# A planner with measured costs for issues and landings, residuals in attention's tiles, and weights cast two ahead, in a two-layer encoder trunk

## The chip, the cores and the metric

The kernel runs on one core of a Trainium2 chip. The metric is device time in microseconds of one execution, lower is better. TensorE (PE) multiplies, VectorE (DVE), ScalarE (ACT) and GpSimd (POOL) do the rest; nearly all transfers are issued by SyncE (SP) into one DMA queue, in its order.

## The reference, cut to what matters

Two sequences (2048 and 512 tokens, width 1024, float32) go through two layers with the same weights.

```python
def even_sublayer(x, w_in, ...):
    u = x @ w_in
    qa, ka, va, za, gd, qb, kb, vb, zb = jnp.split(u, _offsets(EVEN_SPLITS), axis=-1)
    ya = gla_mixer(qa, ka, va, za, gd, ...)    # gated linear attention, both directions, 4 heads of 128
    yb = swa_mixer(qb, kb, vb, zb, ...)        # |i - j| <= 128, 8 query heads, 2 key heads of 64
    return jnp.concatenate([ya, yb], axis=-1) @ w_out

def odd_sublayer(x, w_in, conv_w, w_out):
    u = x @ w_in
    bg, cg, h, z = jnp.split(u, 4, axis=-1)
    t = jnp.pad(cg * h, ((0, 0), (1, 1), (0, 0)))
    conv = conv_w[0] * t[:, :-2] + conv_w[1] * t[:, 1:-1] + conv_w[2] * t[:, 2:]
    return (jax.nn.silu(z) * bg * conv) @ w_out

# each layer
x = layer_norm(DN_ALPHA * x + sub, ln_g[l], ln_b[l])
```

## The kernel before

The 2560 tokens are five groups of 512 (group 4 is the short sequence). A product in float32 precision is made of three products of a rounded format: activations and weights are each split into a high and a low part (`xh`, `xl`; `wh`, `wl`), and xh·wh + xl·wh + xh·wl goes into one PSUM bank (`acc`).

**The dense stream** is TensorE's backbone: stages e1 (input projection of the even layer, 8 weights `w_tok` and 21 weights `w_ch`), oe (its output projection, 8 weights `w_oe`, then residual and LayerNorm to `x1_s`) and odd (32 weights `w_od`, the convolution, 8 weights `w_oo`, residual and LayerNorm to the output). Their order is e1 of groups 4, 3, 2, 1; oe 4; e1 0; odd 4; oe 0; oe 1; odd 0; oe 2; odd 1; oe 3; odd 2; odd 3. A weight tile is 128x1024 and serves 24 matmuls of 512 columns. It is loaded into `ws` (two buffers), cast to its high part `wh` by ScalarE, and the low part `wl` is subtracted by GpSimd in four pieces:

```python
    def cook(self):
        ...
            hi = self.new(self.wp, (128, 1024), F32R, "wh", 2)[:, :n]
            lo = self.new(self.wp, (128, 1024), F32R, "wl", 2)[:, :n]
            nc.scalar.copy(hi, raw)
            for o in range(0, n, n // 4):
                ...
            self.cooked.append((hi, lo))
            self.fetch()

    def weight(self):
        ...
        w = self.cooked.pop(0)
        self.cook()
        return w
```

`weight()` is called where a weight's matmuls begin, so the cast of the next one and the load (`fetch`) of a further one are written there. The load has to wait until the subtraction has read the buffer, and it waits at the head of SP's queue.

**Side streams** are generators that are stepped between groups of dense matmuls (at each `yield` of the dense code, by `Flow.pump`): `prep` and `prep_odd` load a group's activations (`pr`, two buffers), transpose them where needed and split them into `st`; `gla_stream` runs the linear attention in chunks of 128 tokens (tiles `qn`, `tA`, `KK`, `QQ`, `S`, `A`; loads from `k_s`, `q_s`, `qf_s` and so on); `swa_front` and `swa_back` run the windowed attention (`P`, `Q`, `K`, `V`, `mx`, `pth`, `ptl`); `norms` does LayerNorms. PSUM has eight banks: four `acc` for the dense stream, one `psg` for the linear attention, three `pss` for the windowed attention and the transposes.

**The order** of all instructions is fixed when the kernel is built. A small model (`Model`) keeps a clock for every engine, with a cost for each instruction and a landing time for each DMA; a stream's next step is written when the model's TensorE clock has passed the time at which its input is reckoned ready and VectorE and ScalarE are not more than some microseconds ahead. The model's numbers place instructions; on the chip semaphores decide. An instruction placed too early makes its engine wait, with all that stands behind it.

**Residuals and LayerNorm gains.** In `out_ln`, a side stream added where the projection starts waits for the previous projection's LayerNorms, loads gain and offset (`lnf`, `lnb`) and then four or five residual tiles `y` (four buffers, which the LayerNorms before it still use). VectorE adds a finished bank to the residual (`half`), which frees the bank.

Almost every instruction carries line 188, that of the helper which records it; the profile is read by tile names.

Of the kernel before, what the change touches and what calls it, by code (L numbers as in the profile page):

```python
# [96 lines left out]
class Model:  # L97


    def __init__(self):  # L100
        self.clock = dict.fromkeys(("tensor", "vector", "scalar", "gpsimd", "sync"), 0.0)
        self.bus = 0.0
        self.written, self.used, self.free, self.rings = {}, {}, {}, {}
        self.last = 0.0
        self.by, self.dram, self.held = {}, set(), set()

# [10 lines left out]

    def idle(self, name):
        return max(self.written.get(name, (0.0, ""))[0], self.used.get(name, 0.0))

    def alloc(self, tag, old, tile):
        ring = self.rings[tag]
        name = tile.tensor.name
        if old is not None:
            ring.remove(old)
            self.free[name] = self.idle(old)
        ring.append(name)

# [3 lines left out]
    def cost(self, engine, op, outs, ins):  # L132
        n = max(x.free_size() for x in outs + (ins if op != "matmul" else []))
# [6 lines left out]
        if engine == "vector":  # L140
            return n / 960 + 0.155, 0.06
        if engine == "scalar":
            return n / 1250 + 0.21, 0.06
        return n / 480 + 0.3, 0.06

    def note(self, engine, op, outs, ins):
# [21 lines left out]
        for x in outs:  # L168
            if x.tensor.name not in self.dram:
                self.written[x.tensor.name] = (end, engine)  # L170
# [38 lines left out]
class Flow:  # L209
# [5 lines left out]
    AHEAD = 5.0  # L215

    def __init__(self, model):
# [4 lines left out]
        self.late = []  # L222
# [8 lines left out]
    def add(self, gen, ready=0.0):  # L231
        self.side.append([self.t + ready, self.n, gen, None])
        self.n += 1
# [4 lines left out]

    def flush(self, everything=False, name=None):
# [3 lines left out]
        self.late = keep  # L243
# [3 lines left out]
    def drain(self):  # L247
        while self.late:
            self.flush(True)

    def step(self, s):
# [8 lines left out]
        try:  # L260
# [3 lines left out]
            return  # L264
        s[0] = max(self.t, self.model.last)
# [4 lines left out]
        elif said:  # L270
            s[0] = max(s[0], self.model.when(said))

    def room(self):
        c = self.model.clock
        return c["vector"] <= self.t + self.AHEAD and c["scalar"] <= self.t + self.AHEAD - 1.5

    def pump(self):
        self.flush()
        for s in sorted(self.side, key=lambda s: s[:2]):
            if s[0] <= self.t and self.room():  # L280
# [34 lines left out]
class Trunk:  # L315
    def __init__(self, tc, nc, I, y_out, ctx):
# [13 lines left out]
        self.psg = P("psg", 1, space=PSUM)  # L330
        self.pss = P("pss", 3, space=PSUM)
# [18 lines left out]
        self.up_made = False  # L350
# [5 lines left out]
        self.jobs, self.raws, self.cooked = [], [], []  # L356
# [16 lines left out]
    def pd(self, shape=(128, 512), dt=F32):  # L373
        return self.new(self.acc, shape, dt, "acc", 4)

    def pg(self, shape=(128, 512), dt=F32):
        return self.new(self.psg, shape, dt, "psg", 1)

    def pw(self, shape=(128, 512), dt=F32, hold=False):
        return self.new(self.pss, shape, dt, "pss", 3, hold)  # L380

    def m2(self, shape=(128, 512), dt=F32, hold=False):
        return self.new(self.md, shape, dt, "md", 4, hold)
# [6 lines left out]


    def fetch(self):

        if self.jobs:
            src, n = self.jobs.pop(0)
            raw = self.new(self.wp, (128, 1024), F32, "ws", 2)[:, :n]
            self.nc.sync.dma_start(raw, src)
            self.raws.append((raw, n))

    def cook(self):  # L400

        nc = self.nc
        if not self.raws:
            self.fetch()
        if self.raws:
            raw, n = self.raws.pop(0)
            hi = self.new(self.wp, (128, 1024), F32R, "wh", 2)[:, :n]
            lo = self.new(self.wp, (128, 1024), F32R, "wl", 2)[:, :n]
            nc.scalar.copy(hi, raw)
            for o in range(0, n, n // 4):  # L410
                c = slice(o, o + n // 4)
                nc.gpsimd.tensor_tensor(lo[:, c], raw[:, c], hi[:, c].bitcast(F32), op=ALU.subtract)
# [16 lines left out]
    def dense_ch(self, xh, xl):  # L429
# [4 lines left out]
        for k in range(8):  # L434
# [3 lines left out]
            yield  # L438
        for k in range(8):
            c = slice(k * 128, k * 128 + 128)  # L440
            nc.tensor.matmul(p[:], wl[:, c], xh(k), start=False, stop=(k == 7))
            if k % 2 and k < 7:
                yield
        return p

    def dense_tok(self, n, tiles, put):

        nc = self.nc
        out = [(self.pd() if i < 4 else self.pw())[:, :n] for i, t in enumerate(tiles)]
        for kc in range(4):  # L450
# [13 lines left out]
            for i, ((xh, xl), p) in enumerate(zip(tiles, out)):  # L464
                yield from high(xh, xl, p)
                if kc == 3:
                    low(xh, p)
                    put(i, p)
                    yield
            if kc < 3:  # L470
                for (xh, xl), p in zip(tiles, out):
                    low(xh, p)
                    yield

    def log_sig(self, z, out):
# [5 lines left out]
        nc.vector.scalar_tensor_tensor(out, z, 0.0, out, op0=ALU.min, op1=ALU.subtract)  # L481

    def silu(self, z, out, tile, g=None, then=None):

        nc = self.nc
        self.log_sig(z, out)
# [12 lines left out]
        self.flow.defer(rest, tile, z)  # L499
# [26 lines left out]
    def setup_up(self):  # L526

        nc, I = self.nc, self.I
        up = self.new(self.yp, (128, 2, 512), F32R, "y", 4)
        if self.up_made:  # L530
            nc.sync.dma_start(up[:].bitcast(F32), self.up_s)
            return up
        self.up_made = True
# [3 lines left out]
        for d, n in enumerate("bf"):  # L537
            nc.sync.dma_start(raw[:, d], I["up_" + n])
        for d in range(2):
            lo = low[:, d]  # L540
            nc.scalar.copy(hi[:, d], raw[:, d])
# [4 lines left out]
        nc.sync.dma_start(self.up_s, up[:].bitcast(F32))  # L546
        return up

    def setup_late(self):
        nc, c = self.nc, self.const  # L550
# [3 lines left out]
        self.sink = load("sink", (128, 8))  # L554
        self.nsink = c.tile([128, 8], F32, name="nsink")
        nc.vector.tensor_scalar(self.nsink[:], self.sink[:], -1.0, None, op0=ALU.mult)
        self.lmask16 = load("m16", (128, 32), I32)

    def setup_bias(self):
        nc, I, c = self.nc, self.I, self.const  # L560
        self.setup_late()
# [20 lines left out]
        self.bias = c.tile([128, 8, 384], F32, name="bias")  # L582
        b = self.bias_s
        yield 6.0
        nc.sync.dma_start(self.bias[:], bass.AP(b.tensor, b.offset + 127, [[511, 128], [65536, 8], [1, 384]]))
# [6 lines left out]
    def prep(self, key, src, gates):  # L592
# [8 lines left out]
        def get(k):  # L601
            r = self.new(self.md, (128, 512), F32, "pr", 2, True)
            nc.sync.dma_start(r[:], src(k))
            raws.append(r)

        get(0)
        get(1)
        for k in range(8):
            yield raws[:1]
# [9 lines left out]
            if k < 6:  # L619
                get(k + 2)  # L620
        self.flow.mark(key)

    def prep_odd(self, g, gates):
# [10 lines left out]
        def get(hf, t):  # L634
            r = (4 * g + t) * 128
            y = self.new(self.md, (128, 512), F32, "pr", 2, True)
            nc.sync.dma_start(y[:], self.x1_s[r:r + 128, hf * 512:hf * 512 + 512])
            raws.append(y)

        get(*jobs[0])  # L640
        get(*jobs[1])
        for i, (hf, t) in enumerate(jobs):
# [5 lines left out]
            while not self.model.spare("pss", 3):  # L648
                yield 0.5
# [6 lines left out]
            if i < 6:  # L656
                get(*jobs[i + 2])
# [18 lines left out]
    def e1(self, g):  # L676
# [8 lines left out]
        gd = self.sm((128, 4, 32), "gd")  # L685

        def put_v(t, p):
            v = self.m2()
            nc.scalar.copy(v[:, :336], p)
            flow.defer(lambda: nc.sync.dma_start(self.v_s[4 * g + t, :, :336], v[:, :336]), v)  # L690

        def put_r(t, p):
# [6 lines left out]
            nc.vector.tensor_tensor(mk(r, 320, [[64, 2], [1, 64]]), pv, hi, op=ALU.subtract)  # L699
# [4 lines left out]
            flow.defer(store, r)  # L704
# [724 lines left out]
```

## Time and profile before

| | |
|---|---|
| time, median of 3 runs | 2770.91 us (2761.58 to 2774.79) |
| profiled execution | 2769.01 us, span 2767.2 us |
| granted TensorE clock, mean | 0.957 |
| PE busy | 2525.8 us (91%) |
| DVE, ACT, POOL busy | 1429.2, 1208.9, 1236.3 us |
| DMA | 460.42 MB, mean 166 GB/s |

A row of waits "PE acc <- ACT wh" says that TensorE, writing `acc`, stood idle until ScalarE had written `wh`; SPq is SP's queue of DMA issues. A timeline row gives start, duration, engine, operation, tiles out<-in and count, and in brackets the idle time before it with what ended it. Names have their buffer numbers left out.

### The profile page before, as it was taken

Reading aid. Unit: us, or ns where it says so; the run is one execution under the profiler, and the core shown is the slowest. Engines: PE = TensorE matmul, PEld = TensorE weight load, DVE = VectorE, ACT = ScalarE, POOL = GpSimd, SP = SyncE. Lnnn points to the kernel's source line nnn. Section 1 sums busy time; section 2 is a strip of 40 time slices with the busy share of each in tenths; the row PEclk is TensorE's granted clock in tenths of the full one; section 3 lists DMA queues with packets and bytes.
Section 4 is the critical chain, followed back from the end, with each engine's and each line's share of the span. In section 5 each row is a group of like instructions: output and inputs, shape, how many; then the busy total and the mean of one; then the engine's idle time right before and its main releaser. Section 6 shows DMA issues by size and latency. Waiting matters only on the chain. (4 is left out here: it accounts for less than half of the span.)

```text
span 2767.2 us, 43278 instructions
## 1 busy us (share of the span) xinstructions
PE 2525.8 (91%) x16214; PEld 2077.3 (75%) x16214; DVE 1429.2 (52%) x2704; ACT 1208.9 (44%) x2276; POOL 1236.3 (45%) x1552
## 2 busy tenths in 40 slices
PE   6988999898999888999999878997899979989998
PEld 5767778677878677777777667885788758868886
DVE  1246656577777686677866544222433245324324
ACT  2544665555556345564565423332233223333331
POOL 2444434344444343444434544554455435545553
PEclk8999999999999999999999989997999989999999
DMA  4766666474665655655466753334432443234333
GB/s 148 224 204 190 204 220 208 151 232 153 208 204 178 216 178 179 197 164 174 142 219 196 264 200 123 98 98 150 164 122 99 160 167 122 93 111 145 117 99 137
DMA packets 268721, 460.42 MB, mean 166 GB/s; under 512 B 21680, under 2 KB 150448, under 8 KB 268512
## 3 DMA queue, kind: packets, MB, share of 16 engines
q1 hardware_dynamic: 268512, 457.66, 51.2%
q8 instruction: 128, 2.10, 0.3%
q14 instruction: 81, 0.66, 0.1%
HBM read 353.23 MB, written 104.35 MB: 165 GB/s over the span
## 5 line engine op out<-in xcount | busy, mean ns | idle before, releaser
L188 POOL TENSOR_TENSOR wl<-ws,wh 128x256 fp32r<-128x256 f32 (+1 forms) x1524 | 1199.9, 818 | 1476.7 <-ACT wh L188 1320.8
L188 PE MATMUL acc<-st,wh 128*128 128x512 f32 x4240 | 1059.9, 397 | 23.1 <-ACT wh L188 16.4
L188 PEld LDWEIGHTS acc<-st,wh 128*128 128x128 f32 x4240 | 793.3, 190 | 189.3 <-ACT wh L188 19.8
L188 PE MATMUL acc<-st,wl 128*128 128x512 f32 x2120 | 554.9, 396 | 0.0
L188 PE MATMUL acc<-wh,st 128*128 128x512 f32 (+1 forms) x1760 | 441.8, 391 | 71.0 <-DVE y L188 39.4
L188 ACT CAST wh<-ws 128x1024 fp32r<-128x1024 f32 (+1 forms) x381 | 385.5, 1012 | 206.5 <-PE acc L188 146.9
L188 PEld LDWEIGHTS acc<-st,wl 128*128 128x128 f32 x2120 | 395.7, 190 | 78.9
L188 PEld LDWEIGHTS acc<-wh,st 128*128 128x128 f32 x1760 | 335.1, 204 | 125.0 <-issue 37.7
L188 DVE SCALAR_TENSOR_TENSOR md<-acc,md 128x512 f32<-128x512 f32 (+1 forms) x145 | 100.0, 691 | 375.2 <-ACT md L188 354.0
L188 PE MATMUL acc<-wl,st 128*128 128x512 f32 (+1 forms) x880 | 232.0, 385 | 5.6 <-POOL wl L188 5.6
L188 ACT ACTIVATE md<-md 128x512 f32<-128x512 f32 x360 | 226.8, 630 | 11.4 <-DVE md L188 3.6
L188 PEld LDWEIGHTS acc<-wl,st 128*128 128x128 f32 x880 | 164.3, 199 | 33.9 <-POOL wl L188 8.5
L188 ACT ACTIVATE md<-acc 128x512 f32<-128x512 f32 (+1 forms) x165 | 96.8, 596 | 188.0 <-PE acc L188 135.2
L188 DVE SCALAR_TENSOR_TENSOR y<-y,acc 128x512 f32<-128x512 f32 x78 | 53.6, 687 | 168.7 <-PE acc L188 100.5
L188 DVE TENSOR_TENSOR md<-md,acc 128x512 f32<-128x512 f32 x40 | 27.4, 686 | 196.6 <-PE acc L188 196.6
L188 DVE TENSOR_TENSOR md<-acc,md 128x512 f32<-128x512 f32 (+1 forms) x120 | 74.5, 621 | 92.6 <-PE acc L188 58.8
L188 DVE CUSTOM_DVE_ANT_0 P<-pss,bias 128x384 f32<-128x384 f32 (+1 forms) x160 | 83.7, 524 | 58.7 <-PE pss L188 58.0
L188 ACT COPY km<-KK 128x512 f32<-128x512 f32 x80 | 51.1, 639 | 140.1 <-DVE KK L188 140.0
L188 ACT CAST pth<-pss 128x512 fp32r<-128x512 f32 x112 | 65.4, 584 | 105.1 <-PE pss L188 104.9
L188 DVE TENSOR_TENSOR st<-pr,st 128x512 fp32r<-128x512 f32 x80 | 60.1, 758 | 86.4 <-ACT st L188 86.3
L188 ACT ACTIVATE P<-P,nm 128x384 f32<-128x384 f32 (+1 forms) x160 | 93.6, 588 | 10.1 <-DVE nm L188 10.0
L188 ACT CAST st<-md 128x512 fp32r<-128x512 f32 x40 | 24.8, 621 | 165.3 <-DVE md L188 165.3
(151 smaller groups left out, 2595.4 us busy)
## 6 DMA issues: line engine op xcount, KB each, us to landing
ws<-in_w_od SPq DMA_DIRECT2D x160, 512.0 KB, 3.5
ws<-in_w_ch SPq DMA_DIRECT2D x105, 512.0 KB, 3.9
ws<-in_w_oe SPq DMA_DIRECT2D x40, 512.0 KB, 4.3
ws<-in_w_oo SPq DMA_DIRECT2D x40, 512.0 KB, 3.8
ws<-in_w_tok SPq DMA_DIRECT2D x40, 336.0 KB, 3.3
K<-kb_s SPq DMA_DIRECT2D x32, 384.0 KB, 6.5
pr<-in_xT SPq DMA_DIRECT2D x40, 256.0 KB, 4.7
d_s<-md SPq DMA_DIRECT2D x40, 256.0 KB, 4.6
```

What stands on the lines that cost most here:

```text
L188: r = f(*a, **k)
```

## The change

The instructions that compute stay the same; their order, their buffers and the times at which loads are issued change.

- **Estimates** (`Model`). A DMA issue costs SP 0.45 us in place of 0.06, and its data are reckoned to land 3.6 us or more after it in place of 2.2. An operation of VectorE that reads two SBUF tiles is put behind the GpSimd operation that runs at that time (`behind`). A buffer not yet written counts as busy. Some costs differ.
- **Steps.** A stream names the tiles that its next step needs (`yield [Q]`), and is written when those are ready; before, the last operation of the step before counted. `prep`, residuals and LayerNorms go ahead of attention (`rank`), and a stream may take several steps at one point. Operations of the dense code that need another engine's result first (`taps`, `split`, stores) are deferred until it is reckoned done.
- **Weights.** `wh` has three buffers. The high part of a weight is cast two weights ahead, in the middle of a weight's matmuls, the low part at the start of the next weight; the load for a free `ws` buffer is written when the model reckons it free (`fetch_soon`).
- **Residuals.** One stream (`residuals`) loads them stages ahead into any free tile of `y` and, once attention is done with them, `P`, `Q`, `tA`, `QQ`, `KK`. Gain and offset stay in `ln_g`, `ln_b`, and once attention is done in `P` and `Q` too. `pr` has three buffers, and `gb`, `pth`, `ptl` are used for the same purpose at the end of attention; `md` has eight in place of four.
- **PSUM.** `psg` and `pss` become one pool `ps` of four banks; a step waits in the plan until one is reckoned free (`bank`). The dense stream takes a bank of it when its own four are busy.
- The scratch for DMA descriptors is set to 2048 bytes (`dynamic_dma_scratch_size`).

```diff
         if engine == "sync":
-            c[engine] = at + 0.06
+            c[engine] = at + 0.45
             size = max(x.partition_size() * x.free_size() for x in outs) * 4
-            self.bus = max(self.bus, at) + size / 280e3
-            end = max(at + 2.2, self.bus + 1.6)
+            self.bus = max(self.bus, at + 0.45) + size / 280e3
+            end = max(at + 3.6, self.bus + 1.8)
         else:
             cost, more = self.cost(engine, op, outs, ins)
+            if engine == "vector":
+                at = self.behind(at, op, outs, ins)
+            elif engine == "gpsimd":
+                self.pool = self.pool[-12:] + [(at, at + cost)]
...
-    AHEAD = 5.0
+    AHEAD = ((5.0, 5.0), (4.0, 4.0), (4.0, 4.0))
...
-        self.psg = P("psg", 1, space=PSUM)
-        self.pss = P("pss", 3, space=PSUM)
+        self.pside = P("pside", 4, space=PSUM)
...
+    def fetch_soon(self):
+        ...
+        old = self.model.next_free("ws", 2)
+        self.flow.at(self.model.idle(old), go)
+
     def cook(self):
         if not self.raws:
-            self.fetch()
+            if self.coming:
+                self.coming[0]()
+            else:
+                self.fetch()
         if self.raws:
             raw, n = self.raws.pop(0)
-            hi = self.new(self.wp, (128, 1024), F32R, "wh", 2)[:, :n]
-            lo = self.new(self.wp, (128, 1024), F32R, "wl", 2)[:, :n]
-            nc.scalar.copy(hi, raw)
+            hi = self.new(self.wp, (128, 1024), F32R, "wh", 3, True)[:, :n]
+            self.nc.scalar.copy(hi, raw)
+            self.cooking.append((raw, hi, n))
+
+    def cook_low(self):
+        while self.cooking:
+            raw, hi, n = self.cooking.pop(0)
+            lo = self.new(self.wp, (128, 1024), F32R, "wl", 2, True)[:, :n]
             for o in range(0, n, n // 4):
...
             self.cooked.append((hi, lo))
-            self.fetch()
+            self.drop(raw)
+            self.fetch_soon()
 
     def weight(self):
-        if not self.cooked:
-            self.cook()
-        w = self.cooked.pop(0)
-        self.cook()
-        return w
+        self.cook_low()
+        return self.cooked.pop(0)
...
+    def residuals(self, plan):
+        for key, gates, rows, src in plan:
+            for gate in gates:
+                yield gate
+            for i, r in enumerate(rows):
+                while self.free_at(self.large) > self.flow.t or self.model.bus > self.flow.t + 1.0:
+                    yield 0.4
+                y = self.take(self.large, (128, D))
+                self.nc.sync.dma_start(y[:], src[r * 128:r * 128 + 128])
```

What the order becomes, at three places on which the prediction rests. First the start of the program. On SP (loads of the first weights and of x) there stood:

```order
L188 DMA ws<-in_w_tok 128x672
L188 DMA pr<-in_xT 128x512 x2
L188 DMA ws<-in_w_tok 128x672
L188 DMA ident<-in_ident 128x128
L188 DMA hl<-in_hl 128x2
L188 DMA norm_g<-in_norm_g 128x1
L188 DMA ws<-in_w_tok 128x672
L188 DMA pr<-in_xT 128x512 x6
L188 DMA ws<-in_w_tok 128x672 x2
```

and now:

```order
L225 DMA ws<-in_w_tok 128x672
L225 DMA pr<-in_xT 128x512 x2
L225 DMA ws<-in_w_tok 128x672
L225 DMA pr<-in_xT 128x512
L225 DMA md<-in_xT 128x512 x5
L225 DMA ident<-in_ident 128x128
L225 DMA hl<-in_hl 128x2
L225 DMA norm_g<-in_norm_g 128x1
L225 DMA ws<-in_w_tok 128x672 x2
```

The last five loads of x go into `md` tiles, ahead of the constants and of the third weight. On ACT at the same place (casts of weights and of x, before and now):

```order
L188 CAST st<-pr 128x512
L188 CAST wh<-ws 128x672
L188 CAST st<-pr 128x512 x7
L188 CAST wh<-ws 128x672 x4
L188 COPY md<-acc 128x336 x4
```

```order
L225 CAST wh<-ws 128x672
L225 CAST st<-pr 128x512 x3
L225 CAST wh<-ws 128x672
L225 CAST st<-md 128x512 x5
L225 CAST wh<-ws 128x672 x2
```

The second weight's cast moves from behind eight casts of x to behind three; the first stands ahead of all.

Second, SP around the end of odd 4 and the projection oe 0 (`in_x` is the residual of the even layer, `mix_s` the output of attention). Before, the residuals stand inside oe 0, behind the stores of odd 4's LayerNorms:

```order
L188 DMA ws<-in_w_oe 128x1024
L188 DMA out_y<-y 128x1024
L188 DMA pr<-mix_s 128x512
L188 DMA mix_s<-KK 512x1x128
L188 DMA pr<-mix_s 128x512
L188 DMA ws<-in_w_oe 128x1024
L188 DMA out_y<-y 128x1024 x2
L188 DMA lnf<-in_ln_g 128x1024
L188 DMA lnb<-in_ln_b 128x1024
L188 DMA y<-in_x 128x1024 x4
L188 DMA ws<-in_w_oe 128x1024
```

Now residuals go out from the end of odd 4 on, into `P` and `tA`, between the weights:

```order
L225 DMA QQ<-qf_s 128x512
L225 DMA qn<-ga_s 128x512
L225 DMA P<-in_x 128x1024 x2
L225 DMA ws<-in_w_oe 128x1024
L225 DMA ptl<-mix_s 128x512
L225 DMA mix_s<-KK 512x1x128
L225 DMA P<-in_x 128x1024
L225 DMA ws<-in_w_oe 128x1024
L225 DMA mix_s<-qn 512x1x128
L225 DMA pr<-mix_s 128x512
L225 DMA tA<-in_x 128x1024
L225 DMA ws<-in_w_oe 128x1024 x2
```

The residual loads moved ahead of the stores `out_y`, and the loads of gain and offset are gone from this place.

Third, SP at odd 2's output projection (`x_s` is `x1_s`: halves of a group for the next odd layer in `pr`, residuals in `y`). Before:

```order
L188 DMA ws<-in_w_oo 128x1024 x4
L188 DMA pr<-x_s 128x512 x4
L188 DMA ws<-in_w_oo 128x1024
L188 DMA pr<-x_s 128x512 x2
L188 DMA lnf<-in_ln_g 128x1024
L188 DMA lnb<-in_ln_b 128x1024
L188 DMA y<-x_s 128x1024 x4
L188 DMA pr<-x_s 128x512
L188 DMA ws<-in_w_oo 128x1024
L188 DMA pr<-x_s 128x512
L188 DMA ws<-in_w_oo 128x1024 x2
```

Now:

```order
L225 DMA ws<-in_w_oo 128x1024 x3
L225 DMA pr<-x_s 128x512
L225 DMA gb<-x_s 128x512
L225 DMA ws<-in_w_oo 128x1024
L225 DMA gb<-x_s 128x512
L225 DMA pth<-x_s 128x512
L225 DMA ptl<-x_s 128x512
L225 DMA pr<-x_s 128x512
L225 DMA pth<-x_s 128x512
L225 DMA ptl<-x_s 128x512
L225 DMA ws<-in_w_oo 128x1024 x4
```

The loads of x1 go into four kinds of tiles, the residuals are no longer here (they stand ahead of `in_w_oo`, in the last weights of `in_w_od`).

More of the change, by code (lines that the diff above doesn't have):

```diff
@@ L647, in prep_odd @@
             y = raws.pop(0)
-            while not self.model.spare("pss", 3):
-                yield 0.5
+            yield from self.bank()
             pt = self.pw((128, 4, 128), hold=True)
@@ L1146, in swa_back @@
             yield [V, Pt]
-            while self.model.spare("pss", 3) < 2:
-                yield 0.5
+            while self.model.spare("ps", 4) < 2:
+                yield 0.3
+            yield from self.bank()
             po = self.pw(hold=True)
@@ L1156, in swa_back @@
             for kb in range(nk):
-                while not self.model.spare("pss", 3):
-                    yield 0.5
+                yield from self.bank()
                 pt = self.pw((128, 4, 128), hold=True)
```

598 lines of the change are left out of this document (385 added, 213 removed).

## The prediction

> **What bounds the kernel now.** I read the page first, then the stages, the list of waits of TensorE, that of the DMA queue, and last the clock.
>
> ```profile
> span 2767.2 us, 43278 instructions
> PE 2525.8 (91%) x16214; PEld 2077.3 (75%) x16214; DVE 1429.2 (52%) x2704; ACT 1208.9 (44%) x2276; POOL 1236.3 (45%) x1552
> ```
>
> TensorE is busy 91%; no other engine passes 52%. The order of the changed program holds the same 13,447 matmuls, so only two things can move the span: the 2767.2 − 2525.8 = 241.4 us in which TensorE is idle, and the speed at which it runs while busy. The idle time by stage (the columns are the stretch, its length, then the busy time of PE, PEld, DVE, ACT, POOL, the granted clock, DMA share and GB/s):
>
> ```profile
> 0.00:160.00 160.00, 124.08 (x597) 103.48 (x598) 31.51 (x56) 62.30 (x98) 63.18 (x96) 0.88 0.64 201
> 160.00:1030.00 870.00, 801.25 (x7163) 666.66 (x7162) 583.16 (x1200) 471.82 (x933) 361.04 (x444) 0.96 0.62 193
> 1030.00:1560.00 530.00, 501.79 (x3720) 409.91 (x3719) 364.09 (x743) 298.00 (x678) 220.12 (x265) 0.98 0.58 189
> 1560.00:2490.00 930.00, 832.08 (x3572) 678.51 (x3571) 344.63 (x551) 292.01 (x446) 457.08 (x580) 0.94 0.41 135
> 2490.00:2767.20 277.20, 266.62 (x1170) 218.78 (x1168) 105.76 (x156) 84.78 (x123) 134.91 (x168) 0.99 0.37 125
> ```
>
> Length less PE busy gives 35.9 us idle in the first group, 68.8 and 28.2 while attention runs beside the projections, 97.9 in the stretch where only projections and LayerNorms are left, 10.6 at the end. The worst stretch is the one with the least work beside TensorE: it waits for data that is issued late, not for a full engine. What ended the idle time:
>
> ```profile
> PE acc L188 <- ACT wh L188: 43.0, 12, 11.7
> PE acc L188 <- DVE y L188: 39.4, 5, 13.6
> PE pss L188 <- DMA pr<-x_s: 38.6, 9, 8.9
> PE psg L188 <- DMA KK<-k_s: 21.7, 6, 8.3
> PE psg L188 <- DVE QQ L188: 19.1, 7, 5.0
> PE pss L188 <- DVE mx L188: 7.3, 4, 4.4
> PE psg L188 <- DMA QQ<-qf_s: 6.2, 2, 3.8
> PE acc L188 <- POOL wl L188: 5.6, 7, 1.3
> PE acc L188 <- DVE Q L188: 2.1, 1, 2.1
> SPq L188 <- POOL wl L188: 1121.3, 367, 6.1
> SPq L188 <- ACT wh L188: 683.1, 292, 10.5
> ```
>
> Each row names the engine and the tile it writes, what it waited for, the total in us, how often and the longest. The last two rows are the DMA queue's own. It stands still for 1121.3 + 683.1 = 1804 us, 65% of the span, behind a weight load whose buffer GpSimd or ScalarE still reads; what is queued behind that load (a residual, a chunk of attention) is late by as much.
>
> Clock is lost as well. This is the sum over the 37 stretches in which the granted clock stood at one half (length, then busy times):
>
> ```profile
> sum 236.58, PE 162.36 PEld 132.01 DVE 86.65 ACT 52.13 POOL 73.87; mean PE 4.39 PEld 3.57 DVE 2.34 ACT 1.41 POOL 2.00
> ```
>
> PE was busy 162.36 us there and did half as much as at full speed: 81 us lost. Idle and clock together hold 241 + 81 = 322 us, and with everything gone the span would be 2445 us.
>
> **The change, part by part.** The sum goes against the profiled execution, 2769.0 us (span 2767.2 and 1.8 around it); the median of the runs, 2770.9, lies 1.9 above it.
>
> (a) Weights, 43.0 + 5.6 = 48.6 us. Before, the cast of a weight's high part goes out when the weight before it starts; now it goes out two thirds through the weight ahead of that, into a third buffer. A weight is 24 matmuls, and undisturbed they take 192.03 / 846 = 0.227 us each, 5.4 us; the cast takes 1.0 us and the four subtractions behind it 4 × 0.82 = 3.3 us.
>
> ```profile
> 2509.05 192.03 PE acc L188 x846
> L188 POOL TENSOR_TENSOR wl<-ws,wh 128x256 fp32r<-128x256 f32 (+1 forms) x1524 | 1199.9, 818 | 1476.7 <-ACT wh L188 1320.8
> L188 ACT CAST wh<-ws 128x1024 fp32r<-128x1024 f32 (+1 forms) x381 | 385.5, 1012 | 206.5 <-PE acc L188 146.9
> ```
>
> So what may stand ahead of a cast on ScalarE before TensorE stops grows from 5.4 − 1.0 = 4.4 us to 1.8 + 5.4 − 1.0 = 6.2 us; the subtractions keep theirs, being needed two thirds of a weight later. The largest wait of the row is at the start:
>
> ```profile
> 9.37 10.86 SPq L188 DMA_DIRECT2D pr<-in_xT  x6
> 23.80 1.40 ACT L188 CAST wh<-ws 128x672 fp32r<-128x672 f32 x2
> 24.60 4.57 PE L188 MATMUL acc<-wh,st 128*128 128x336 f32 x16 [11.72 <-ACT wh L188]
> ```
>
> The six loads of x took 10.86 us to issue, since two buffers pass them on; the cast of the second weight stood behind all eight casts of x. Now all eight loads are issued before anything waits (first place below the change), and the second weight's cast stands behind three. The first load and cast can't go (6.3 us before the first matmul), and I leave 8 us for the rest, half of it for x that lands late at the start. Remain 14 of 48.6: 34.6 saved.
>
> (b) Residuals, 39.4 us. The one of 13.65 us:
>
> ```profile
> 1581.85 0.90 SPq L188 DMA_DIRECT2D out_y<-y  x2
> ...
> 1584.95 4.92 SPq L188 DMA_DIRECT2D y<-in_x  x4
> 1594.17 0.69 DVE L188 SCALAR_TENSOR_TENSOR y<-y,acc 128x512 f32<-128x512 f32 x1 [13.34 <-DMA y<-in_x]
> 1595.01 5.22 PE L188 MATMUL acc<-wh,st 128*128 128x512 f32 x14 [13.65 <-DVE y L188]
> ```
>
> The four residuals wait for the four y tiles that the last LayerNorms still write out, then for the gains; they land 9 us after the issue, and meanwhile the sums in PSUM can't be emptied. Now they are issued one stage ahead into tiles that attention has left (second place), tens of matmuls ahead of their use, and gain and offset stay resident. That is five waits whose cause is gone; I leave 2 us: 37.4 saved. VectorE is next in line there and idle enough (344.63 of 930 us busy).
>
> (c) Loads behind a standing queue: 38.6 (x1 for the odd layers), 21.7 (k) and 6.2 (q), 66.5 us. Typical:
>
> ```profile
> 2456.70 12.83 SPq L188 DMA_DIRECT2D ws<-in_w_oo  x3
> 2469.58 10.57 SPq L188 DMA_DIRECT2D pr<-x_s  x4
> 2473.78 1.09 PE L188 MATMUL pss<-ident,pr 128*128 128x128 f32 x4 [8.88 <-DMA pr<-x_s]
> pr<-x_s SPq DMA_DIRECT2D x40, 256.0 KB, 4.2
> ```
>
> Three weight loads hold the queue for 12.83 us, the transposes stand in TensorE's order as if x1 were there. The change queues a weight load only when its buffer is reckoned free, reckons 0.45 us for an issue and at least 3.6 us for a landing where it had 0.06 and 2.2, and spreads x1 over nine buffers in place of two (third place). Against the median landing of 4.2 us the new reckoning is nearly right; loads that take longer will still be awaited for 1 to 2 us. I keep a fifth, 13 us: 53.5 saved. What is moved in the queue is moved past the stores too (v, vb, out_y), and those are read a stage later.
>
> (d) The rest of the waits is 241.4 − 48.6 − 39.4 − 66.5 − 8.5 = 78.4 us; 8.5 us is the tail after the last matmul, which the change leaves alone:
>
> ```profile
> 2735.53 23.21 PE acc L188 x101
> ```
>
> This last run of matmuls ends at 2735.53 + 23.21 = 2758.7 of 2767.2. The 78.4 us are steps of attention placed before their input is there (19.1 and 7.3 above, the others under 6 each) and such things as the end of an odd stage, where the carried columns must be made first (the row of 2.1). In the new order a step is placed when its named input is reckoned done, no longer when the last operation of its stream is, and VectorE is reckoned later where GpSimd is at work. Unknown is how good that is: nothing back if the new estimates are as wrong as the old, all back at best. I take a half, 39 us: each step is covered by dense matmuls in the meantime, but the end of an odd stage has no such cover and stays. New mistakes of the order I put at 10 us, between 0 and as much as (d) held.
>
> (e) The clock. Half-clock stretches come with waits:
>
> ```profile
> 196.00:206.00 10.00, 7.70 (x94) 5.85 (x93) 3.12 (x5) 3.91 (x6) 3.52 (x4) 1.00 0.56 178
> 498.32 0.50 PE L188 MATMUL acc<-y 128*128 128x512 f32 x1 [1.51 <-ACT y L188]
> 499.75:503.16 3.41, 3.41 (x10) 2.65 (x9) 0.17 (x1) 3.35 (x10) 2.63 (x4) 0.50 0.00 0
> 1585.18:1598.84 13.66, 3.83 (x9) 3.09 (x10) 2.75 (x4) 0.00 (x0) 2.27 (x4) 0.50 0.91 367
> ```
>
> The first stretch holds 2.3 us of idle time and kept the full clock. The matmul in the second row came after 1.51 us of waiting, and the 3.41 us behind it ran at half speed. The last is the wait under (b). Waits fall from 233 (241.4 less the tail) to 14 + 2 + 13 + 39 + 10 = 78 us, to a third; as short ones remain and some of them cost clock, I keep 40% of 81 us: 48 saved; the ends are 0 and 81. The Trainium skill ("TensorE: Matmul & The Clock Gate", section "HAM oscillation — how this bites in real kernels") gives as the abstract rule "no PE-idle gaps >~3.4µs". By that rule the short waits that remain would cost no clock, and I estimate that some 20 us more would come back, still inside my forecast. The trace agrees only in part: ahead of the stretch at 499.75 stood no such gap.
>
> (f) What I cost at nothing. The side streams' four PSUM banks were one for the linear attention and three for the windowed; as one pool they let either stream run when the other has no need, and a step waits for a bank in the plan, under dense matmuls. The descriptor scratch made smaller only frees SBUF: the transfers go through the hardware queue.
>
> ```profile
> q1 hardware_dynamic: 268512, 457.66, 51.2%
> ```
>
> Sum: 34.6 + 37.4 + 53.5 + 39 − 10 + 48 = 202.5. Time 2769.0 − 202.5 = 2566; the median of the runs would put it 2 us higher, which I don't resolve.
>
> **Rivals.**
> 1. *Half of it.* The large waits go, but each is followed by a smaller one of the same stage, since TensorE comes sooner and loads then collide; (a) to (c) give half (63), (d) nothing, and the clock a quarter (20): 2769 − 83 = 2686. For it: DMA already takes 0.62 of its engines in the second stretch. Against: residuals move by a whole stage, which no estimate can spoil.
> 2. *Nearly all of it.* Only the start, the tail and three ends of odd stages (2.1 us each) remain idle, clock lost 10: 2445 + 6.3 + 8.5 + 6.3 + 10 + 1.8 = 2478. For it: no other engine is above 70% in any stretch.
> 3. *Slower: the weight buffers turn too slowly.* A raw buffer is loaded (3.5 us), cast (1.0) and subtracted (3.3), with the issue 0.4: 8.2 us, and two buffers must give a weight each 5.4 us, so 10.9 us per turn. Before, the next load stood in the queue and left the moment the buffer was free; now it leaves when the plan thinks so. If that is later by d, TensorE waits (d − 2.7) / 2 for each of the 381 weights. It has eaten the 202 us at d = 3.8 us and ends slower beyond that; d = 5 costs 438 us and gives 3004 us. Against it: a weight that is needed and not loaded is issued at once, and the plan's costs are near the rows.
>
> ```profile
> ws<-in_w_od SPq DMA_DIRECT2D x160, 512.0 KB, 3.5
> ```
>
> 4. *No change.* The order differs, the waits only move: within 0.5% (14 us, about what a measurement of this kernel can tell).
>
> **Numbers.** The forecast, 2500 to 2625, has 0.57; half of it (2625 to 2755) 0.21; nearly all (below 2500) 0.10; no change 0.04; slower 0.08. Faster is then 0.88. The range 2475 to 2690 leaves out the slower case, no change and the worst part of rival 1.
>
> **What would show it.** (a) PE <- ACT wh below 12 us; (b) the row PE <- DVE y gone; (c) PE waits on DMA below 20 us together, and the queue's waits for POOL wl far under 1121; (d) idle time of the second and third stretch halved; (e) a granted clock of 0.97 or more in the stretch that now has 0.94. I am wrong if weight loads are awaited in every stage, if the queue still stands, or if idle time moves to attention's PSUM banks, which are now one pool of four.

## The result and the profile after

The changed kernel takes 2506.15 us (median of 4 runs, 2504.23 to 2507.69) against 2770.88 us in the runs beside it (2761.58 to 2774.79): a ratio of 0.9049, interval 0.9025 to 0.9073. The profiled execution took 2504.69 us, with a mean granted clock of 0.994. First the span and the busy times, from the head of the page:

```profile
span 2502.9 us, 43603 instructions
PE 2445.0 (98%) x16214; PEld 2028.8 (81%) x16214; DVE 1456.4 (58%) x2710; ACT 1210.8 (48%) x2276; POOL 1248.2 (50%) x1552
```

TensorE is idle for 2502.9 − 2445.0 = 57.9 us in place of 241.4, so 183.5 us came back from waits. Its busy time fell by 2525.8 − 2445.0 = 80.8 us with the same number of instructions. The same stretches as before (length, then the busy times of PE, PEld, DVE, ACT, POOL, granted clock, DMA share, GB/s; the work in them is not quite the same, as everything comes earlier now):

```profile
0.00:160.00 160.00, 150.72 (x917) 126.24 (x918) 55.92 (x89) 86.85 (x136) 88.49 (x122) 1.00 0.78 243
160.00:1030.00 870.00, 842.58 (x7721) 704.41 (x7720) 618.53 (x1319) 509.69 (x1019) 381.50 (x471) 0.99 0.66 209
1030.00:1560.00 530.00, 523.14 (x3452) 431.33 (x3452) 374.26 (x701) 282.76 (x657) 261.46 (x304) 1.00 0.62 205
1560.00:2490.00 930.00, 924.17 (x4111) 763.50 (x4110) 399.40 (x591) 330.49 (x461) 516.72 (x656) 1.00 0.39 131
2490.00:2502.90 12.90, 4.37 (x20) 3.29 (x18) 8.29 (x11) 1.00 (x4) 0.00 (x0) 0.85 0.24 97
```

Idle are 9.3, 27.4, 6.9 and 5.8 us, and 8.5 at the end; before it was 35.9, 68.8, 28.2, 97.9 and 10.6. What TensorE waited for, and below it the DMA queue (total, times, longest):

```profile
PE acc L225 <- ACT st L225: 6.3, 1, 6.3
PE ps L225 <- DVE QQ L225: 6.1, 7, 3.0
PE acc L225 <- ACT wh L225: 5.0, 3, 2.4
PE ps L225 <- ACT A L225: 4.3, 1, 4.3
PE acc L225 <- DMA gb_s<-md: 4.2, 1, 4.2
PE acc L225 <- DVE K L225: 4.1, 2, 2.1
PE acc L225 <- POOL wl L225: 3.8, 5, 1.1
SPq L225 <- POOL wl L225: 1196.6, 325, 8.7
SPq L225 <- ACT wh L225: 77.3, 73, 3.6
```

The first row is the lead before the first matmul, 6.3 us as before the change. The waits for loads (x1, k, q) and for residuals are gone, from these rows and from those below them; the one DMA row is for a store (`gb_s<-md`) that is read back. The queue still stands for 1196.6 + 77.3 = 1274 us behind weight loads, 51% of the span (before 1804 us, 65%).

The clock: the sum over the seven stretches at half clock, the last of which is the tail (length, busy times):

```profile
sum 29.83, PE 20.63 PEld 17.41 DVE 14.25 ACT 11.81 POOL 13.61; mean PE 2.95 PEld 2.49 DVE 2.04 ACT 1.69 POOL 1.94
```

TensorE was busy 20.63 us there: 10 us lost in place of 81. So the 264.3 us between the spans are 183.5 of idle time, 71 of clock, and 10 that I can't assign.

### The profile page after: what moved, and what is told of

The parts are those of the page before. It is cut to its first block, busy times and chain, and to the rows that moved or that the text cites. A ratio compares the mean times of both kernels' runs of the same rounds, so it can differ in the third digit from the quotient of the medians.

```text
span 2502.9 us, 43603 instructions
## 1 busy us (share of the span) xinstructions
PE 2445.0 (98%) x16214; PEld 2028.8 (81%) x16214; DVE 1456.4 (58%) x2710; ACT 1210.8 (48%) x2276; POOL 1248.2 (50%) x1552
## 4 chain that ended last, share of the span: by engine, by line
PE 85%; DVE 6%; DMA 4%; ACT 2%; POOL 1%; issue 1%; SPq 1%; DVEq 0%; ACTq 0%; POOLq 0%
PE acc L225 71%; PE ps L225 14%; DVE KK L225 1%; DVE QQ L225 1%; POOL wl L225 1%; DVE P L225 1%; DMA ws<-in_w_ch 1%; DMA ws<-in_w_tok 1%; SPq L225 1%; ACT wh L225 1%; DVE st L225 1%; DMA qb_s<-md 0%; DVE md L225 0%; DVE y L225 0%; ACT P L225 0%
## 5 line engine op out<-in xcount | busy, mean ns | idle before, releaser
L225 PEld LDWEIGHTS acc<-st,wh 128*128 128x128 f32 x4160 | 768.3, 188 | 156.1 <-ACT wh L225 3.4
L225 PE MATMUL acc<-wh,st 128*128 128x512 f32 (+1 forms) x1648 | 387.1, 372 | 14.4 <-ACT st L225 6.3
L225 PEld LDWEIGHTS acc<-wh,st 128*128 128x128 f32 x1648 | 293.0, 190 | 59.3 <-ACT wh L225 7.2
L225 ACT ACTIVATE md<-md 128x512 f32<-128x512 f32 x315 | 197.6, 631 | 33.0 <-DVE md L225 26.3
L225 PE MATMUL acc<-wl,st 128*128 128x512 f32 (+1 forms) x824 | 207.7, 370 | 3.9 <-POOL wl L225 3.8
L225 ACT CAST pth<-ps 128x512 fp32r<-128x512 f32 x112 | 65.1, 581 | 71.1 <-PE ps L225 66.3
L225 DVE CUSTOM_DVE_ANT_0 P<-ps,P 128x384 f32<-128x384 f32 (+1 forms) x160 | 79.4, 525 | 29.9 <-PE ps L225 28.9
L225 DVE TENSOR_TENSOR ptl<-ps,pth 128x512 fp32r<-128x512 f32 x112 | 76.2, 681 | 6.3 <-ACT pth L225 6.0
L225 PE MATMUL ps<-K,Q 128*128 128x384 f32 (+1 forms) x320 | 74.1, 339 | 3.6 <-DVE mx L225 2.7
L225 DVE TENSOR_SCALAR P<-P,den 128x384 f32<-128x384 f32 (+1 forms) x160 | 73.7, 519 | 1.4
```

What stands on the lines that cost most here:

```text
L225: r = f(*a, **k)
```

## The experiments

Two theories. **A:** the lead over the loads comes from the estimates of the title (a DMA issue of 0.45 us, a landing of 3.6). **B:** it comes from where the weight loads stand in SP's queue: written when the plan reckons their buffer free (`fetch_soon`), no longer right behind the subtraction, so that other loads go ahead of them. Further theories take one part each: the residual's tiles, the casts two ahead, the PSUM pool, the rules of the plan. Each kernel ran in 3 rounds beside the kernel before. Since those runs were in four groups, on three chips, kernels are compared by their ratios; 0.0010 is 2.8 us. Kernels whose plans differ little came out at 0.8918 to 0.9054 (e7, e11, e1, e10), so a difference of some 20 us between two plans is not by itself the worth of one part.

| kernel | us | ratio | interval |
|---|---|---|---|
| after | 2506.2 | 0.9049 | 0.9025 to 0.9073 |
| e1 after, old DMA estimates | 2500.7 | 0.9022 | 0.9008 to 0.9035 |
| e10 after, all estimates old | 2507.8 | 0.9054 | 0.9032 to 0.9075 |
| e2 before, new DMA estimates | 2749.9 | 0.9916 | 0.9893 to 0.9940 |
| e3 after, weight loads written at once | 2564.0 | 0.9253 | 0.9237 to 0.9269 |
| e5 before, weight loads written later | 2655.9 | 0.9575 | 0.9545 to 0.9605 |
| e9 before, whole weight part | 2702.8 | 0.9761 | 0.9733 to 0.9788 |
| e6 after, cast one ahead | 2526.4 | 0.9104 | 0.9077 to 0.9132 |
| e4 after, few residual tiles | 2520.4 | 0.9092 | 0.9078 to 0.9106 |
| e12 after, PSUM banks split | 2529.2 | 0.9130 | 0.9115 to 0.9145 |
| e8 after, old rules of the plan | 2512.8 | 0.9053 | 0.9026 to 0.9080 |
| e7 after, steps wait for the last operation | 2475.0 | 0.8918 | 0.8887 to 0.8949 |
| e11 as e7, old DMA estimates | 2497.6 | 0.9016 | 0.8994 to 0.9038 |

### The estimates: e1, e2, e10

e1 puts the old numbers for a DMA into the changed kernel:

```diff
-            c[engine] = at + 0.45
+            c[engine] = at + 0.06
...
-            self.bus = max(self.bus, at + 0.45) + size / 280e3
-            end = max(at + 3.6, self.bus + 1.8)
+            self.bus = max(self.bus, at) + size / 280e3
+            end = max(at + 2.2, self.bus + 1.6)
```

> The changed kernel with the old estimates of a DMA alone (issue 0.06 us, landing 2.2 us and 1.6 after the bus), all else as changed. Theory A (lead): loads come in time because they are reckoned to land later, so that they are written further ahead of their use; then TensorE's waits on DMA come back, 30 to 60 us of them, with clock, and the time is 2560 to 2620 us. Theory B (queue): they come in time because weight loads no longer hold the head of the queue; then the time stays below 2525 us.

Not slower: 0.9022. One load of x1 is late by 8.0 us where none was (the waits of TensorE, largest row), and the rest makes up for it. Theory A falls for the changed kernel.

```profile
PE ps L225 <- DMA ptl<-x_s: 8.0, 1, 8.0
```

e2 does the reverse, the new numbers in the kernel before:

```diff
-            c[engine] = at + 0.06
+            c[engine] = at + 0.45
...
-            self.bus = max(self.bus, at) + size / 280e3
-            end = max(at + 2.2, self.bus + 1.6)
+            self.bus = max(self.bus, at + 0.45) + size / 280e3
+            end = max(at + 3.6, self.bus + 1.8)
```

> The kernel before with the new estimates of a DMA alone (0.45, 3.6, 1.8). Theory A: the rows of TensorE's waits on pr, KK and QQ fall from 66.5 us to below 25, the clock gains, and the time is 2670 to 2720 us. Theory B: the queue stands as before, the waits stay above 50 us and the time within 20 us of 2771.

It gains 0.8%, some 23 us, which is neither theory's figure: less than A's 50 us, and just more than B's 20. The wait for x1 stays and that for k falls from 21.7 to 3.5 us (last row), but waits for VectorE and ScalarE in attention rise. The queue's wait for `wh` is 679.0 us (before 683.1):

```profile
PE acc L188 <- ACT wh L188: 40.4, 14, 11.2
PE pss L188 <- DMA pr<-x_s: 39.6, 8, 8.7
PE acc L188 <- DVE y L188: 31.5, 6, 11.7
PE psg L188 <- DVE acmp L188: 29.2, 20, 4.8
PE psg L188 <- DMA KK<-k_s: 3.5, 3, 2.4
```

e10 sets back all estimates: e1's edit, the old costs of VectorE and ScalarE, and no delay behind GpSimd.

```diff
-            return n / 960 + (0.155 if len(outs) < 2 else 0.23), 0.06
+            return n / 960 + 0.155, 0.06
...
-                at = self.behind(at, op, outs, ins)
+                pass
```

> The changed kernel with all old numbers in the model: DMA, engine costs, and no waiting of VectorE behind GpSimd. Theory E (the measured numbers carry a part, as the change is named after them): steps are placed too early again, DVE and ACT waits of attention return, 2540 us or more. Rival S (structure does it, not numbers; the old DMA numbers alone cost nothing): 2490 to 2520 us.

0.9054, no difference from the changed kernel. With the rest of the change in place, the measured numbers bring nothing that can be seen.

### Where the weight loads stand: e3, e5, e9

e3 writes the load at once, in `cook_low`, and leaves all else:

```diff
-            self.fetch_soon()
+            self.fetch()
```

> The changed kernel, but a weight load is written at once when the last subtraction from its buffer is written, as before the change, so that it stands at the head of the queue. Theory A: loads have lead enough, time within 15 us of 2506. Theory B: the queue stands 600 us longer, waits on DMA of 30 us and more return, 2560 us or more.

0.9253, some 57 us above the changed kernel with the intervals far apart: the largest loss of any part undone. The waits of TensorE and of the queue:

```profile
PE ps L225 <- DMA pth<-x_s: 21.3, 3, 18.6
PE ps L225 <- ACT km L225: 20.9, 4, 9.3
SPq L225 <- POOL wl L225: 1453.9, 354, 8.8
SPq L225 <- ACT wh L225: 160.1, 125, 5.9
```

The queue stands 1614 us, 63% of its span of 2567.5. That is 340 us longer than in the changed kernel, where theory B had 600. A late x1 and late steps of attention are back, and TensorE is idle for 107.3 us in place of 57.9.

e5 gives `fetch_soon` alone to the kernel before, with the raw buffer held until it is subtracted:

```diff
     def cook(self):
         if not self.raws:
-            self.fetch()
+            if self.coming:
+                self.coming[0]()
+            else:
+                self.fetch()
...
-            self.fetch()
+            self.fetch_soon()
```

> The kernel before with one part of the change alone: the load of a weight is written when its buffer is reckoned free. Theory B (the place of weight loads in the queue is the main cause): TensorE's waits on DMA fall from 66 us to below 30, with clock, and the time is 2680 to 2720 us; the queue's waits for ScalarE's cast (683 us) fall to below 200. Theory C (the parts need each other: with two weight buffers a later load only makes the cast later): no faster than 2755 us, waits on ACT wh grow.

0.9575: 4.25% or some 118 of the 264 us by one call, with the hold that it needs. It went further than both theories had it.

```profile
PE acc L188 <- ACT wh L188: 53.2, 11, 9.4
PE pss L188 <- DMA pr<-x_s: 26.7, 6, 14.9
PE acc L188 <- DVE y L188: 22.2, 3, 9.8
SPq L188 <- POOL wl L188: 846.5, 309, 5.3
SPq L188 <- ACT wh L188: 486.6, 219, 13.4
```

The queue stands 1333 us, 50% of 2660.2. I expected its wait for `wh` below 200 us; it is 486.6, as the cast is still written late. The wait for k (21.7 us before) is gone, x1 and residuals have lost a third and nearly half, and the wait for `wh` itself has grown (43.0 to 53.2).

e9 adds the rest of the weight part to that: a third `wh`, the high part cast two ahead, the low part at the next weight's start, and the small descriptor scratch:

```diff
-            hi = self.new(self.wp, (128, 1024), F32R, "wh", 2)[:, :n]
+            hi = self.new(self.wp, (128, 1024), F32R, "wh", 3, True)[:, :n]
...
-        w = self.cooked.pop(0)
-        self.cook()
-        return w
+        self.cook_low()
+        return self.cooked.pop(0)
...
+                if i == 2:
+                    self.cook()
```

> The kernel before with the whole weight part of the change and nothing else: later loads, a third buffer for high parts, casts two ahead, the low part at the next weight's start. Theory Q (the queue is the main cause and the later cast adds to it): waits on ACT wh fall from 53.2 us (later loads alone) to below 25, and the time is 2600 to 2640 us. Rival (the casts matter only with the rest of the change): within 15 us of 2656, which later loads alone gave.

0.9761, some 51 us slower than e5, which neither theory had. The row that it aims at did fall, but those of attention rose:

```profile
PE psg L188 <- DVE acmp L188: 29.0, 18, 7.4
PE psg L188 <- ACT km L188: 28.8, 10, 8.7
PE acc L188 <- ACT wh L188: 20.4, 6, 6.8
1424.00:1640.00 216.00, 150.99 (x966) 117.79 (x966) 150.47 (x328) 105.71 (x343) 35.99 (x44) 0.80 0.64 209
```

The last row is a stretch as above. GpSimd, which prepares the weights, is busy for 36 of 216 us: few dense matmuls are left to place, and the last steps of attention, which oe 0 needs, run one behind the other at a granted clock of 0.80. The dense stream had come there sooner than attention. So a part that works alone can lose when another bound lies next; the queue stands only 46% here, so that share is not by itself a measure of the time.

### One part undone: e6, e4, e12

e6 has two `wh` buffers and casts a weight at the start of the one before it:

```diff
-            hi = self.new(self.wp, (128, 1024), F32R, "wh", 3, True)[:, :n]
+            hi = self.new(self.wp, (128, 1024), F32R, "wh", 2, True)[:, :n]
...
+        w = self.cooked.pop(0)
+        self.cook()
...
-                if i == 2:
-                    self.cook()
```

> The changed kernel with the cast of a weight where it was, at the start of the weight before, and two buffers for high parts. Theory W (casts two ahead carry a large part, since the later load needs the slack): waits on ACT wh and POOL wl grow from 8.8 us to 40 us or more, the clock falls, 2560 us or more. Rival, the prediction's reckoning of spare time (4.4 us against 6.2): 10 to 20 us slower, below 2530 us.

0.9104, some 15 us slower. TensorE's wait for the cast is small, though the queue's wait for it is back; one load of x1 is late as well:

```profile
PE acc L225 <- ACT wh L225: 12.1, 7, 4.3
PE ps L225 <- DMA pr<-x_s: 9.6, 1, 9.6
SPq L225 <- ACT wh L225: 409.5, 216, 5.4
```

e4 takes the borrowed tiles away from the residuals (`KK` stays, which lies free after attention):

```diff
-        self.large += [(self.e2, n, 1) for n in ("tA", "QQ", "KK")]
+        self.large += [(self.e2, n, 1) for n in ("KK",)]
...
-        self.large += places
```

> The changed kernel with residuals in the four y tiles and one of attention's alone, so that they must wait for the LayerNorms before them as before the change. Theory R (the buffers carry term b): the waits on DVE y return, 25 to 40 us, with 15 to 25 us of clock: 2545 to 2570 us. Rival: issuing them by a stream of its own ahead of attention is enough: below 2520 us.

0.9092, some 12 us, the intervals just apart: far from theory R's 2545, and at the edge of its rival's 2520. Of the 40 residual loads 33 go into `y` here, yet TensorE waits for `y` only once, 1.7 us; VectorE waits for a residual, mostly under other work:

```profile
DVE y L225 <- DMA y<-in_x: 12.8, 4, 6.5
```

e12 splits the pool: one bank for the linear attention, with its own wait in the plan, three for the rest.

```diff
-        self.pside = P("pside", 4, space=PSUM)
+        self.pside = P("pside", 3, space=PSUM)
+        self.psg = P("psg", 1, space=PSUM)
```

> The changed kernel with the side streams' banks as before: one for the linear attention, three for windowed attention and transposes; all else as changed. Theory L (the common pool is what lets attention finish in time): attention falls behind, the output projection of group 0 waits for it as in the run with the weight part alone, idle time between 1030 and 1560 us rises from 6.9 to 40 us or more, and the time is 2560 us or more. Rival: placing steps by named inputs and several at a time is enough, 2495 to 2530 us, inside the scatter of equal plans (2475 to 2508).

0.9130, some 22 us. Theory L's marks (40 us idle, 2560 us) were not reached; the time is at the upper end of its rival's 2495 to 2530. It loses where e9 did: the third stretch (1030 to 1560 us) is idle for 24.6 us in place of 6.9, with steps of the linear attention one behind the other before oe 0 (two rows of the timeline; in brackets the idle time before):

```profile
1429.88 1.35 PE L225 MATMUL psg<-ident,km 128*128 128x128 f32 x4 [6.93 <-ACT km L225]
1441.62 1.35 PE L225 MATMUL psg<-ident,km 128*128 128x128 f32 x4 [7.53 <-ACT km L225]
```

### The rules of the plan: e8, e7, e11

e8 sets back the ranks, the lead allowed to VectorE and ScalarE, and one step per pump:

```diff
-    AHEAD = ((5.0, 5.0), (4.0, 4.0), (4.0, 4.0))
+    AHEAD = ((5.0, 3.5), (5.0, 3.5), (5.0, 3.5))
...
-        self.side.append([self.t + ready, self.n, gen, None, 0 if first else rank])
+        self.side.append([self.t + ready, self.n, gen, None, 0])
...
-            while s in self.side and s[0] <= self.t and self.room(s[4]):
-                if s[3] is not None and s[3] not in self.done:
-                    break
+            if s[0] <= self.t and self.room(s[4]):
```

> The changed kernel with the old policy of the streams: no ranks, one step at a point, VectorE 5 us and ScalarE 3.5 us ahead at most. Theory P (ranks and several steps carry a part of b and d): loads and LayerNorms come behind attention's steps, 30 us or more slower, 2540 us or more. Rival: below 2520 us.

0.9053: nothing that can be told from the changed kernel. Theory P falls.

e7 lets a stream's next step wait for its last operation too, as before the change:

```diff
-            s[0] = max(self.t, self.model.when(said))
+            s[0] = max(self.t, self.model.last, self.model.when(said))
```

> The changed kernel, but a step of a stream is written no earlier than when the last operation of its step before is reckoned done, besides the tiles it names. Theory N (named inputs carry term d): placing steps later gives more cover, not less, so no slower by this alone unless attention runs out of time; 2495 to 2525 us. Rival: attention's chains get too long, the output projections wait for them, 2540 us or more.

2474.99 us (2473.11 to 2478.79), 0.8918: some 36 us faster than the changed kernel by the ratios, with the intervals apart, and the fastest here. Neither theory had that.

```profile
PE acc L225 <- ACT st L225: 6.7, 1, 6.7
PE acc L225 <- ACT wh L225: 4.8, 3, 2.3
PE acc L225 <- DVE K L225: 4.1, 2, 2.1
PE acc L225 <- POOL wl L225: 3.2, 5, 1.2
PE ps L225 <- DMA pr<-x_s: 2.7, 2, 2.3
160.00:1030.00 870.00, 859.01 (x7888) 720.19 (x7878) 644.76 (x1383) 531.77 (x1065) 392.31 (x482) 1.00 0.68 217
```

The waits for `QQ`, `A`, `gb_s` and `mx` have left the top of the list, the stretch with attention is idle for 11.0 us in place of 27.4, and but for the lead no wait passes 3 us. e11 has the edits of e7 and e1 together:

> The changed kernel with steps no earlier than the last operation of the step before (2475 us by itself) and the old DMA numbers (2501 us by themselves against 2506). If the two gains add, 2465 to 2472 us; if the earlier reckoning of landings only moved attention's steps, which the first edit settles already, 2472 to 2480 us or worse.

The gains do not add: 0.9016, with one late load that e7 has not:

```profile
PE ps L225 <- DMA pr<-x_s: 13.0, 2, 10.4
```

e7 and e11 differ only in the plan's estimates of a DMA, and by 27 us (by the ratios). Such an estimate goes into the place of every load, and here one load fell badly. So the 12 to 22 us of e4, e6 and e12, and a good part of e7's gain, may lie in the particular order as much as in the part that was changed; that was not separated.

## Why the prediction was right, and where not

The direction held, and the largest mechanism with it: weight loads that hold the queue, and late loads behind them (e3 and e5, from both sides). The forecast of 2566 lay 60 us too high, and the measured 2506 lies only 6 us inside the lower end of the range (2500 to 2625). Three kernels with small edits of the plan came out at 2475 (e7), 2498 (e11) and 2501 us (e1): that this plan fell inside is partly luck. A slip that changes nothing: the 13,447 matmuls stand in no trace; both have 16,214 records. Step by step:

- **(a) Weights.** Forecast to remain 14, marker `wh` below 12: measured 5.0 + 3.8 + 6.3 (the lead, now the row of `st`) = 15.1 us, and `wh` 5.0. The start went as told; these rows answer the one of 24.60 us:

```profile
9.40 0.75 ACT L225 CAST wh<-ws 128x672 fp32r<-128x672 f32 x1
12.46 2.61 PE L225 MATMUL acc<-wh,st 128*128 128x336 f32 x16
```

  e6 lies where the reckoning of spare time had it (10 to 20 us slower), but TensorE's waits for `wh` and `wl` make up only 9.3 us of that (8.8 to 18.1); the late x1 is new. So two casts ahead are not shown to be the whole term. In the kernel before, the rest of the weight part takes the wait for `wh` from 53.2 (e5) to 20.4 us (e9).
- **(b) Residuals.** The row is gone, as forecast. That the borrowed tiles do it was not borne out: without most of them (e4) 1.7 us come back. What does it (the earlier issue, gains that stay resident, the queue) was not separated; e5 shows that later weight loads alone take 17 of the 39 us.
- **(c) Loads.** The marker for TensorE held: its waits on DMA are 4.2 us together (forecast below 20). The marker for the queue was wrong. I said the waits for `wl` would fall far below 1121 us; they are 1196.6, and the wait for `wh` fell instead (683.1 to 77.3). That the queue still stands was even named as a sign that I am wrong. It stands 1314 us in e7, the fastest kernel, and 1244 us in e9, so its standing time is no measure of the time; that it hurts only when a load that is needed stands behind is the likely reason, not shown by itself. And the step that put part of the gain on the new estimates (0.45 and 3.6 us) failed: e1 and e10 show nothing for them. TensorE waits for x1 8 to 13 us in the three kernels with the old ones (e1, e10, e11), but also 10 to 16 us in e6 and e8, which have the new.
- **(d) The rest, and new mistakes.** (c), (d) and new mistakes were to leave 13 + 39 + 10 = 62 us; left are 57.9 less 15.1 and the tail of 8.5, that is 34. The idle time of the second and third stretch fell by 60% and 76%, more than the half forecast. The half was too little, and e7 shows that the rule I credited here, a step placed when its named input is ready, is not the reason: without it the second stretch is idle for 11.0 us in place of 27.4.
- **(e) The clock.** The mechanism held, the size not: of 81 us I kept 33, and 10 are left. The fourth stretch stands at 1.00 (forecast 0.97 or more). This term, 71 in place of 48, and the idle time, 183.5 in place of 154.5, carry the error: 23 + 29 of 60 us; the rest is what I can't assign. The rule quoted from the Trainium skill ("TensorE: Matmul & The Clock Gate", section "HAM oscillation — how this bites in real kernels") came out nearer in the sum, with its 20 us more, though the prediction does not show how they were reached. As a limit it does not fit the trace: below, a wait of 2.41 us cost clock.
- **(f) Nothing.** As a cost it was nothing. As a gain it may not be: e12's split loses some 22 us, which is within what two plans can differ by, and the same waits for `km` stand in e3, which has the one pool. So the pool's part is not shown. The smaller descriptor scratch was tried only within e9.

Rival 3, weight buffers that turn too slowly, did not come: TensorE waits 8.8 us for weights in all. What the rivals missed is that attention's last steps before oe 0 become the next bound (e9 and e12, and in e3 the 20.9 us for `km`).

How the whole adds up stays partly open. Undone singly, the parts cost 57 + 22 + 15 + 12 us, those of e8 and e10 nothing, and e7's gains 36: no more than 106 of 264. That parts stand in for each other is a guess. Not tried singly were the deferred operations of the dense code, the larger number of `pr` and `md` tiles, the start, the resident gains, and the descriptor scratch.

## What to carry to other kernels

Where one in-order queue feeds everything, first ask what stands behind a load whose buffer isn't free: writing that load later, in one call, brought 118 us here, against 23 us for better estimates of a DMA (e5 and e2, each alone in the kernel before). Look next for the step that the faster stream will run into (here the end of attention), since a change that is good alone can lose there. And a planner's output should be measured in several variants: the estimates of a DMA moved this one by 27 us, and a simpler rule (e7) came out ahead of the finer one.

## What the runs showed of the hardware

The same wait does not always cost clock. Three matmuls of the changed kernel follow (in brackets the wait before each), and below them the half-clock stretches near by (granted clock in the third column from the end):

```profile
198.49 0.93 PE L225 MATMUL acc<-wh,st 128*128 128x336 f32 x2 [2.41 <-ACT wh L225]
1950.71 0.51 PE L225 MATMUL acc<-wh,K 128*128 128x512 f32 x1 [2.07 <-DVE K L225]
2218.03 0.51 PE L225 MATMUL acc<-wh,K 128*128 128x512 f32 x1 [2.07 <-DVE K L225]
198.41:201.82 3.41, 3.33 (x42) 2.91 (x42) 1.75 (x3) 1.60 (x3) 3.11 (x6) 0.50 0.14 20
2219.10:2222.51 3.41, 3.41 (x12) 2.73 (x12) 0.69 (x1) 0.59 (x1) 0.00 (x0) 0.50 0.77 264
```

At the first a stretch of 3.41 us at half clock begins, and some 1 us after the third another; the second, after the same 2.07 us as the third, has none near by. So waits of 2 to 2.5 us sometimes cost clock and sometimes not, in the same program; what decides was not tried. Second, the clock lost went with TensorE's idle time from kernel to kernel. With half of PE's busy time in the half-clock stretches as the loss, idle times of 241, 192, 176, 107, 58 and 39 us (before, e9, e5, e3, after, e7) went with losses of 81, 58, 40, 26, 10 and 3 us.
